# Eight result loads made in place and ahead of the last gate projections, in a hybrid mLSTM and differential-attention block

## The chip, the cores and the metric

The kernel runs on one core of one Trainium2 chip, as one launch. The metric is the device time of the whole program in microseconds (us). The three runs of the kernel before took 1701.33, 1698.94 and 1702.51 us; their median is 1701.33. All profile rows come from one more execution, taken by the hardware profiler.

## The reference, cut to what matters

One layer on a sequence of 1024 positions and a width of 1024, in float32. Two branches are computed from the same normalised input, each is gated, and their sum goes through an output projection:

```
proj = rmsnorm(x) @ w_in            # split into a_q, a_k, a_v, a_o, a_z, a_g, b_q, b_k, b_v, b_z, g_a, g_b
y_a  = rmsnorm(mlstm_fw + mlstm_bw) * sigmoid(a_o) * silu(a_z)          # branch A, 4 heads
y_b  = rmsnorm(diff_attention(rope(b_q), rope(b_k), b_v)) * silu(b_z)   # branch B, 8 heads
mix  = sigmoid(g_a + gb[0]) * (y_a @ w_branch_a) + sigmoid(g_b + gb[1]) * (y_b @ w_branch_b)
out  = rmsnorm(x + mix @ w_out)
```

The gates are the two sigmoids in front of the branch products. The kernel writes a sigmoid as a tanh of half its argument.

## The kernel before, in words

Every float32 matrix product is made of three products of rounded halves: each operand is held as a high part (written H, a rounded copy) and a low part (written L, the operand less its high part), and the products H·H, H·L and L·H are added up in PSUM. So every operand that comes from DRAM has to be split first: ScalarE copies it to H, and VectorE subtracts H from it to get L (for weights, GpSimd does the subtraction).

The work runs in stages. First the normalised input is split and stays in SBUF as hH and hL. Then come most input projections, the eight heads of branch B (whose results go to the DRAM tiles `yb`), and the four heads of branch A (whose results go to the DRAM tiles `ya`). The 16 gate projections, eight for each branch, are used as filler for TensorE throughout. One of them (`gate_units`) is two products of 24 matmuls, one for each half of the sequence; ScalarE takes each half's tanh from PSUM into the tile `gt`, of which there is one buffer (line 1547), and a DMA stores it to DRAM. PSUM holds two buffers `pj` for all these products, so a product can only start when the product two before it has been read by ScalarE or VectorE.

Three gate projections, called `rest`, are left when branch A's last head ends. The first five pieces of the 48 that they are cut into (a piece is three matmuls) run before that head's last transposes, the list `late`; seven more stand with `late`; then the pool w2 of branch A's heads is given back and the pool wy takes its place. From there the last 36 pieces are woven with eight calls of `load_y`, one for each of the eight 128-row tiles of branch B's result. A call loads a tile of 128 x 1024 float32 into a staging buffer `yraw` (two of them), ScalarE copies it to a slot H, and VectorE writes the low part to a slot L; both are slots of the tag `yb`, which has 16.

After the last gate product the memory of hH and hL is given back to the pool wr. Then pass B (`mix_units("gb")`) multiplies the eight loaded tiles with `w_branch_b`: 8 output tiles x 2 halves x 8 input tiles x 3 matmuls, input tile 0 first. VectorE multiplies each half by the gate, which is loaded back into `tgl`. Branch A's first four tiles are loaded by the same `load_y` into slots of the tag `r` in wr; branch A's last four go to slots of the tag `yb` that pass B has left. Pass A, the output projection and the last norm follow.

The order of TensorE's instructions is the program's order from here on (`keep(E.PE)`). The other engines' orders, and that of the DMA queue of SyncE (SP), are set by the planner, which puts an instruction where its own model of time has its operands ready, and of several ready ones takes the one that stands first in the program. Once built, each engine and each queue runs strictly in its order: an instruction that waits holds all behind it. Nearly every DMA of the kernel is issued by SP; six gate stores of the opening are issued by ScalarE. A tile of wy waits only for those tiles of w2 whose memory it takes.

Of the kernel before, what the change touches and what calls it, by code (L numbers as in the profile page):

```python
# [7 lines left out]
F32 = mybir.dt.float32  # L8
# [6 lines left out]
S = 1024  # L15
# [4 lines left out]
L = 256  # L20
# [25 lines left out]
class Unit:  # L46
# [5 lines left out]
    def __init__(self, cost, fn, keys=(), tag=None, hold=0.0, name=None, after=(), lane=0):  # L52
        self.cost, self.fn, self.keys = cost, fn, keys
        self.tag, self.hold, self.name, self.after, self.lane = tag, hold, name, after, lane
# [55 lines left out]
class Block:  # L110
    def __init__(self, tc, A):
        self.tc, self.nc, self.A = tc, tc.nc, A
        nc = self.nc
        self.v, self.a, self.p, self.t, self.q = nc.vector, nc.scalar, nc.gpsimd, nc.tensor, nc.sync
        self.wt = {}
        self.raws = {}
        self.ml, self.opening, self.ahead, self.terms, self.forms = False, True, False, {}, 0
        self.rs, self.tk, self.loaded = {}, {}, set()
        for n in ("w1", "w2", "wy", "wr"):
            setattr(self, n, _Late(self, "_" + n))  # L120
        self.gc = {}
# [709 lines left out]
    def gate_units(self, seg, i):  # L831
        key = ("w_in", OFF[seg] + 128 * i)
        idx = (0 if seg == "ga" else 8) + i

        def done(half, ps):
            t = self.wpool.tile([128, 512], F32, name="gt", tag="gt")
            self.a.activation(out=t, in_=ps, func=AF.Tanh, scale=0.5, bias=self.gbh[:, idx:idx + 1])
            (self.a if self.opening else self.q).dma_start(out=self.tg[seg][i][:, half * 512:(half + 1) * 512], in_=t)
        return sum((self.proj(key, half, lambda ps, half=half: done(half, ps)) for half in range(2)), [])


# [465 lines left out]
        return un, prev["O"](0) + prev["g"](1) + prev["scale"](4) + prev["scale"](6) + prev["O"](1)  # L1307


    def load_y(self, src, i, slot):  # L1310
        raw = self.wy.tile([128, S], F32, name="yraw", tag="yraw", bufs=2)
        self.q.dma_start(out=raw, in_=src[i])
        h, l = slot("H"), slot("L")
        self.a.copy(h, raw)  # L1314
        self.v.tensor_tensor(out=l, in0=raw, in1=h.bitcast(F32), op=ALU.subtract)  # L1315
        return h, l

    def slot(self, which, dt=F32R):
        pool, bufs = {"yb": (self.wy, 16), "mb": (self.wy, 8), "r": (self.wr, 16)}[which]
        return pool.tile([128, S], dt, name="sl_" + which, tag=which, bufs=bufs)  # L1320
# [108 lines left out]
    def build(self):  # L1429
# [19 lines left out]
        do = lambda f, cost=0.0: Unit(cost, f)  # L1449
        pool = lambda *x, **k: tc.tile_pool(*x, **k)  # L1450
        with pool(name="const", bufs=1) as self.const, \
# [32 lines left out]
            gq = [("gb", i) for i in range(8)] + [("ga", i) for i in range(8)]  # L1484
            fill = lambda m: sum((self.gate_units(*gq.pop(0)) for _ in range(m)), [])
# [16 lines left out]
            st3 = {}  # L1502
            w = Weaver()
            w.add(enter("h", "hpool"), enter("tab", "tab", side="right"), enter("tf", "tf", side="right"),
                  enter("p0", "p0", side="right"), banks("ps0", T=6), keep(E.PE, E.Activation, E.DVE, E.Pool), do(begin))
            k = self.PIECES
# [60 lines left out]
            w.add(enter("w2", "w2", side="right"), banks("ps2", T=2, SS=1, PO=1, I=1))  # L1567
            ml, late = self.ml_units([self.ml_head(n, stm[n]) for n in range(NH_A)], fill(2))
            w.add(do(lambda: setattr(self, "ml", True)), *ml)
            rest = fill(len(gq))  # L1570
            cut = len(rest) // 4
            w.add(*rest[:5])
            w.weave(late, rest[5:cut])
            w.add(do(lambda: setattr(self, "ml", False)), leave("ps2", "w2"), enter("wy", "wy", side="right"))
            yb = lambda x: self.slot("yb")
            loads = [do(lambda k=k: st3.__setitem__(("gb", k), self.load_y(self.yb, k, yb)), 1.0) for k in range(8)]
            w.weave(loads, rest[cut:])

            w.add(leave("h"), enter("wr", "wr"))
            passB = self.mix_units("gb", st3)  # L1580
# [1 line left out]
            loads = [do(lambda k=k: st3.__setitem__(("ga", k), self.load_y(self.ya, k, r)), 1.0) for k in range(4)]  # L1582
            w.add(*passB[:len(passB) // 2])
            w.weave(loads, passB[len(passB) // 2:])
            w.add(*[do(lambda k=k: st3.__setitem__(("ga", k), self.load_y(self.ya, k, yb))) for k in range(4, 8)])
            passA = self.mix_units("ga", st3)
            loads = [do(lambda k=k: self.load_wo(k, st3, "yb"), 1.0) for k in range(3)]
            k = len(passA) // 2
# [52 lines left out]
```

## Time and profile before

| | |
|---|---|
| median of 3 runs | 1701.33 us (1698.94 to 1702.51) |
| the profiled execution's own time | 1699.79 us |
| its span, first to last instruction | 1698.0 us |
| TensorE busy | 1650.1 us, 97% |
| mean granted TensorE clock | 0.996 |
| VectorE, ScalarE, GpSimd busy | 994.1, 760.0, 635.3 us |
| DMA | 178.79 MB, mean 105 GB/s |

Matmuls are pipelined and the profiler models their ends, so the distance from one start to the next is what counts: 0.227 us for a matmul of 512 columns at the full clock in the gate products and in pass B. PE is TensorE, PEld its weight loads, DVE VectorE, ACT ScalarE, POOL GpSimd; SPq and ACTq are the DMA issues of SyncE and ScalarE. Times in rows are us from the start of the span.

### The profile page before, as it was taken

The numbers are of one execution on the slowest core, as the hardware profiler recorded it, in microseconds if no ns is written. First come the engines' busy times: TensorE is split into PE (matmuls) and PEld (weight loads), VectorE is DVE, ScalarE is ACT, GpSimd is POOL, SyncE is SP. The second block draws the span as 40 slices with busy tenths as digits, with TensorE's granted clock in tenths as the row PEclk, the third lists the DMA queues.
The fourth block names the chain that finished last, engine by engine and source line by source line (L and its number), as shares of the span: only waits on it lengthen the run. The fifth ranks groups of instructions, "written<-read, shape, count | busy, mean of one in ns | idle before, by whom it ended". The sixth has DMA issues, their size and how long they took to land. (4 is left out here: it accounts for less than half of the span.)

```text
span 1698.0 us, 25367 instructions
## 1 busy us (share of the span) xinstructions
PE 1650.1 (97%) x9431; PEld 1387.7 (82%) x9431; DVE 994.1 (59%) x1799; ACT 760.0 (45%) x1522; POOL 635.3 (37%) x712
## 2 busy tenths in 40 slices
PE   7999999999999999999999999999999898999998
PEld 5777887887888988898888888889999777888887
DVE  5778668674277666766666765126666644135533
ACT  6454555543254454454445454325656644022221
POOL 5767676665343235424351431221331311212000
PEclk9999999999999999999999999999999999999999
DMA  5334434434231213221230221175554327344222
GB/s 179 101 118 134 137 115 134 124 124 137 75 81 44 63 38 87 63 63 37 76 88 26 63 75 63 50 208 155 143 170 140 104 93 244 119 142 136 87 92 83
DMA packets 175630, 178.79 MB, mean 105 GB/s; under 512 B 12185, under 2 KB 135410, under 8 KB 175506
## 3 DMA queue, kind: packets, MB, share of 16 engines
q1 hardware_dynamic: 174594, 175.58, 34.5%
q8 instruction: 74, 1.21, 0.3%
q10 hardware_dynamic: 912, 1.59, 0.2%
q14 instruction: 50, 0.41, 0.1%
HBM read 114.11 MB, written 46.24 MB: 94 GB/s over the span
## 5 line engine op out<-in xcount | busy, mean ns | idle before, releaser
L429 PE MATMUL pj<-hH,wH 128*128 128x512 f32 x640 | 266.3, 416 | 3.3 <-ACT f L542 1.5
L429 PE MATMUL pj<-hH,wL 128*128 128x512 f32 x640 | 251.9, 394 | 1.7 <-POOL wL L207 1.7
L429 PE MATMUL pj<-hL,wH 128*128 128x512 f32 x640 | 250.6, 392 | 0.2 <-DVE hL L580 0.2
L209 POOL TENSOR_TENSOR wL<-raw,wH 128x1024 fp32r<-128x1024 f32 x41 | 99.6, 2429 | 284.2 <-ACT wH L204 281.8
L928 ACT ACTIVATE e<-S,nm 128x1024 f32<-128x1024 f32 x128 | 142.7, 1115 | 134.2 <-DVE nm L926 133.9
L948 DVE TENSOR_TENSOR pL<-T,pH 128x512 fp32r<-128x512 f32 x128 | 87.9, 688 | 117.4 <-ACT pH L947 116.7
L926 DVE TENSOR_REDUCE nm<-S 128x1 f32<-128x1024 f32 x128 | 150.5, 1217 | 10.1 <-PE S L923 9.3
L429 PEld LDWEIGHTS pj<-hH,wH 128*128 128x128 f32 x640 | 120.7, 189 | 37.8 <-issue 14.4
L451 PE MATMUL pj<-wH,hH 128*128 128x256 f32 x512 | 149.9, 293 | 1.6 <-DVE vL L1035 1.3
L451 PE MATMUL pj<-wL,hH 128*128 128x256 f32 x512 | 144.9, 283 | 1.4 <-POOL wL L207 1.4
L429 PEld LDWEIGHTS pj<-hH,wL 128*128 128x128 f32 x640 | 120.4, 188 | 30.1 <-POOL wL L207 3.1
L451 PE MATMUL pj<-wH,hL 128*128 128x256 f32 x512 | 144.5, 282 | 0.0
L429 PEld LDWEIGHTS pj<-hL,wH 128*128 128x128 f32 x640 | 121.0, 189 | 18.2 <-DVE hL L580 0.6
L429 PE MATMUL pj<-sl_yb,wH 128*128 128x512 f32 x384 | 121.8, 397 | 4.7 <-ACT sl_yb L1314 2.1
L947 ACT CAST pH<-T 128x512 fp32r<-128x512 f32 x128 | 74.7, 584 | 100.5 <-PE T L131 99.9
L204 ACT CAST wH<-raw 128x1024 fp32r<-128x1024 f32 x56 | 58.8, 1050 | 126.8 <-PE pj L429 86.4
L923 PE MATMUL S<-kst,qq 64*128 64x512 f32 x768 | 106.5, 408 | 0.0
L451 PEld LDWEIGHTS pj<-wH,hH 128*128 128x128 f32 x512 | 97.7, 191 | 6.8 <-issue 3.9
L451 PEld LDWEIGHTS pj<-wL,hH 128*128 128x128 f32 x512 | 97.5, 190 | 2.3 <-POOL wL L207 2.3
L451 PEld LDWEIGHTS pj<-wH,hL 128*128 128x128 f32 x512 | 97.7, 191 | 0.1
L429 PEld LDWEIGHTS pj<-sl_yb,wH 128*128 128x128 f32 x384 | 73.3, 191 | 22.8 <-DVE sl_yb L1315 3.3
L934 DVE SCALAR_TENSOR_TENSOR e<-e,r,e 128x1024 f32<-128x1024 f32 x64 | 88.8, 1388 | 2.2
(358 smaller groups left out, 4099.9 us busy)
## 6 DMA issues: line engine op xcount, KB each, us to landing
raw<-in_w_in_dram SPq DMA_DIRECT2D x88, 512.0 KB, 3.8
kst<-hl SPq DMA_DIRECT2D x64, 128.0 KB, 2.4
qq<-hl SPq DMA_DIRECT2D x64, 128.0 KB, 2.4
x<-in_x_dram SPq DMA_DIRECT2D x8, 512.0 KB, 6.2
cak<-y SPq DMA_DIRECT2D x16, 256.0 KB, 2.3
cakH<-cin SPq DMA_DIRECT2D x16, 256.0 KB, 4.4
cakL<-tz SPq DMA_DIRECT2D x16, 256.0 KB, 4.0
gm<-oz SPq DMA_DIRECT2D x16, 256.0 KB, 2.8
```

The source lines that it names most:

```text
L204: self.a.copy(wH, raw)
L209: self.p.tensor_tensor(out=wL, in0=raw, in1=wHf, op=ALU.subtract)
L429: self.t.matmul(ps, lhsT=l[:, k, :], rhs=r, start=(n == 0), stop=(n == 23))
L451: self.t.matmul(ps[:, i, :], lhsT=l, rhs=r[:, k, :], start=(kh == 0 and k == 0 and m == 0), stop=(kh == 1 and k == 3 and m == 2))
L923: self.t.matmul(ps[:, o], lhsT=qq[r, x, c], rhs=k[r, y, o], start=(m == 0), stop=(m == 2))
L926: v.tensor_reduce(out=nm, in_=ps, axis=AX.X, op=ALU.max, negate=True)
L928: a.activation(out=e, in_=ps, func=AF.Exp, bias=nm[:, 0:1], accum_out=Z[:, j, t:t + 1])
L934: v.scalar_tensor_tensor(out=e0, in0=e, scalar=r[:, 0:1], in1=e0, op0=ALU.mult, op1=ALU.add)
L947: a.copy(pH[:, :, s], ps)
L948: v.tensor_tensor(out=pL[:, :, s], in0=ps, in1=pH[:, :, s].bitcast(F32), op=ALU.subtract)
```

## The change

`load_y` gets a form without staging: the DMA writes straight into the slot L (seen as plain float32), ScalarE copies from there to H, and VectorE subtracts in place. Branch B's eight loads and branch A's first four use it; branch A's last four keep the staging buffer. Branch B's eight loads now all stand ahead of the remaining pieces of `rest` instead of being woven among them. A flag `last`, set at the head of `rest`, makes ScalarE instead of SP issue the six stores of the last three gates; setting it is a unit of its own at the front of the list `rest`, which thus has 49 entries where it had 48, and is cut at the same places.

```diff
-        self.rs, self.tk, self.loaded = {}, {}, set()
+        self.rs, self.tk, self.loaded, self.last = {}, {}, set(), False
...
-            (self.a if self.opening else self.q).dma_start(out=self.tg[seg][i][:, half * 512:(half + 1) * 512], in_=t)
+            (self.a if self.opening or self.last else self.q).dma_start(out=self.tg[seg][i][:, half * 512:(half + 1) * 512], in_=t)
...
-    def load_y(self, src, i, slot):
-        raw = self.wy.tile([128, S], F32, name="yraw", tag="yraw", bufs=2)
-        self.q.dma_start(out=raw, in_=src[i])
-        h, l = slot("H"), slot("L")
+    def load_y(self, src, i, slot, direct=True):
+
+        if direct:
+            h, l = slot("H"), slot("L")
+            raw = l.bitcast(F32)
+            self.q.dma_start(out=raw, in_=src[i])
+        else:
+            raw = self.wy.tile([128, S], F32, name="yraw", tag="yraw", bufs=2)
+            self.q.dma_start(out=raw, in_=src[i])
+            h, l = slot("H"), slot("L")
         self.a.copy(h, raw)
         self.v.tensor_tensor(out=l, in0=raw, in1=h.bitcast(F32), op=ALU.subtract)
...
-            rest = fill(len(gq))
+            rest = [do(lambda: setattr(self, "last", True))] + fill(len(gq))
             cut = len(rest) // 4
             w.add(*rest[:5])
             w.weave(late, rest[5:cut])
...
-            w.weave(loads, rest[cut:])
+            w.add(*loads, *rest[cut:])
...
-            w.add(*[do(lambda k=k: st3.__setitem__(("ga", k), self.load_y(self.ya, k, yb))) for k in range(4, 8)])
+            w.add(*[do(lambda k=k: st3.__setitem__(("ga", k), self.load_y(self.ya, k, yb, False))) for k in range(4, 8)])
```

## Rows read from the trace of the kernel before

**Rows 1.** The page's busy times: engine, us, share of the span, instructions.

```profile
PE 1650.1 (97%) x9431; PEld 1387.7 (82%) x9431; DVE 994.1 (59%) x1799; ACT 760.0 (45%) x1522; POOL 635.3 (37%) x712
```

**Rows 2.** The chain that ended last: start, duration, what; the stretch around pass B's start.

```profile
1414.70 6.32 DMA yraw<-yb
...
1423.39 4.89 DMA yraw<-yb
...
1430.65 81.82 PE pj L429 x350
```

**Rows 3.** Timeline of TensorE: start, duration, line, operands, count; in brackets idle before, releaser.

```profile
1419.55 0.39 PE L429 MATMUL pj<-hH,wL 128*128 128x512 f32 x1
1420.90 0.72 PE L429 MATMUL pj<-sl_yb,wH 128*128 128x512 f32 x2 [0.96 <-ACT gt L837]
...
1424.90 0.39 PE L429 MATMUL pj<-sl_yb,wL 128*128 128x512 f32 x1
1426.27 0.49 PE L429 MATMUL pj<-sl_yb,wH 128*128 128x512 f32 x1 [0.99 <-ACT sl_yb L1314]
1427.53 0.50 PE L429 MATMUL pj<-sl_yb,wH 128*128 128x512 f32 x1 [0.76 <-DVE sl_yb L1315]
...
1429.39 0.80 PE L429 MATMUL pj<-sl_yb,wH 128*128 128x512 f32 x1 [1.13 <-ACT sl_yb L1314]
1430.65 0.80 PE L429 MATMUL pj<-sl_yb,wH 128*128 128x512 f32 x1 [0.46 <-DVE sl_yb L1315]
...
1436.36 0.63 PE L429 MATMUL pj<-sl_yb,wH 128*128 128x512 f32 x2
```

**Rows 4.** Stretches: length, busy us by engine (instructions), granted clock, DMA share, GB/s.

```profile
1425.00:1430.00 5.00, 2.12 (x6) 0.77 (x4) 1.85 (x2) 2.09 (x2) 0.62 (x1) 0.90 0.91 255
1430.00:1432.00 2.00, 1.54 (x4) 1.16 (x4) 0.69 (x2) 0.00 (x0) 0.00 (x0) 0.50 0.79 263
...
1436.00:1438.00 2.00, 2.00 (x11) 1.63 (x10) 0.99 (x1) 0.00 (x0) 0.00 (x0) 1.00 0.59 231
```

**Rows 5.** Timeline of ScalarE in the last two gate products.

```profile
1408.87 1.05 ACT L204 CAST wH<-raw 128x1024 fp32r<-128x1024 f32 x1 [2.95 <-PE pj L429]
...
1419.21 1.05 ACT L1314 CAST sl_yb<-yraw 128x1024 fp32r<-128x1024 f32 x1 [6.03 <-DMA yraw<-yb]
1420.16 0.68 ACT L837 ACTIVATE gt<-pj,gbh 128x512 f32<-128x512 f32 x1
```

**Rows 6.** Waits of SP's queue, 1396 to 1431 us: total, times, longest.

```profile
SPq L1312 <- DVE sl_yb L1315: 9.9, 8, 2.3
SPq L838 <- ACT gt L837: 6.9, 2, 5.8
```

**Rows 7.** Timeline of SP: the first load of branch B's results.

```profile
1398.23 0.37 SPq L1312 DMA_DIRECT2D yraw<-yb  x1
```

**Rows 8.** Instructions on tile yraw: duration ns min/median/max, first and last start.

```profile
L1314 ACT CAST sl_yb<-yraw x12: 1044/1052/1057, 1402.1 to 1518.3; 128x1024 fp32r<-128x1024 f32 x12
L1315 DVE TENSOR_TENSOR sl_yb<-yraw,sl_yb x12: 1211/1224/2635, 1403.2 to 1519.8; 128x1024 fp32r<-128x1024 f32 x12
```

**Rows 9.** Stretches again, for the DMA rate in the last column.

```profile
1406.00:1410.00 4.00, 4.00 (x19) 3.33 (x18) 1.17 (x1) 1.13 (x2) 0.00 (x0) 1.00 1.01 366
...
1398.00:1420.00 22.00, 21.93 (x97) 17.83 (x95) 6.22 (x4) 8.84 (x10) 4.80 (x2) 1.00 0.85 285
1414.00:1431.00 17.00, 12.70 (x50) 8.99 (x49) 5.57 (x5) 6.33 (x7) 2.49 (x1) 0.94 0.82 249
```

**Rows 10.** Instructions on tile gt in the opening: the stores that ScalarE issued.

```profile
L838 ACTq DMA_DIRECT2D tgb<-gt x6: 326/326/358, 25.0 to 60.9; - x6
```

**Rows 11.** Instructions on tile gt, 1395 to 1431 us: how long its stores took.

```profile
DMA to landing us min/median/max: 5.1/5.1/5.2
```

**Rows 12.** Timeline of TensorE at branch A's last transposes.

```profile
1386.07 0.39 PE L429 MATMUL pj<-hH,wL 128*128 128x512 f32 x1
1386.97 1.96 PE L131 MATMUL T<-ident,hm 128*128 128x128 f32 x8 [0.52 <-ACT hm L1216]
```

## The prediction, made before the change was run

> **What bounds the kernel now.** I read the page's busy times first: TensorE is busy 97% of the span [rows 1], so only time in which it waits or runs slowly can be won. The chain that ended last says where that is around this change: it is matmuls up to about 1409 us, then for some 20 us loads of `yraw` with their splits, then 82 us of matmuls without a break [rows 2]. So the loads of branch B's results end last at the start of pass B. The timeline of TensorE shows what this costs [rows 3]. The last gate matmul starts at 1419.55. The first matmul of pass B could follow 0.227 us later, at 1419.78 (0.227 is the distance of matmul starts at the full clock), but starts at 1420.90: its PSUM buffer was still to be read. Input tiles 0 to 5 run until 1424.90; tiles 6 and 7 come in four steps, each held by ScalarE's or VectorE's half of a split. From 1430.65 nothing waits, but the engine is on the lower of its two clock levels: the granted clock is 0.50 (1.2 GHz) in 1430 to 1432 and 1.00 (2.4 GHz) again in 1436 to 1438, behind a stretch of 5 us in which TensorE was busy for 2.12 [rows 4].
>
> **What the stall is worth.** Up to 1436.36, pass B has done 36 matmuls (24 of its first product and 4 x 3 of its second). At the full clock from 1419.78 they take 36 x 0.227 = 8.2 us and end at 1427.9. They ended 8.4 us later. That splits into 1.1 us for the PSUM buffer (1419.78 to 1420.90), 4.6 us in the steps for tiles 6 and 7 (1425.13 to 1430.65 is 5.5 us, in which four matmuls of 0.9 us together were started), 2.5 us by the low clock (from 1430.65 the 14 matmuls took 5.7 us, where 14 x 0.227 is 3.2), and 0.2 in slightly longer distances before. The size 8.4 is sure; the split matters only if a part of it stays.
>
> **Why the loads are late, and what the edits do to that.** Three holds stand in a ring. (1) Two `yraw` buffers: SP waited 9.9 us, in 8 waits, for VectorE to finish a split before it could issue the next load [rows 6]. (2) SP's order: gate stores stood among the loads, and SP waited 6.9 us in two of them for the tanh that they store [rows 6]. (3) ScalarE's order: the tanh of a gate product that ended at about 1414.3 stood behind a cast that waited 6.03 us for its load, and ran only at 1420.16 [rows 5]; that is the late PSUM buffer.
>
> Loads in place take hold (1) away: each of the eight has its own slot, so SP can issue them one after the other. Stores issued by ScalarE take (2) away. The first load was issued at 1398.23, in 0.37 us [rows 7], right behind branch A's last stores; from there eight issues take about 3 us, to 1401.3. Their bytes are 8 x 128 x 1024 x 4 = 4.2 MB. In front of them are branch A's last two stores (0.5 MB) and beside them, in ScalarE's row, up to three gate stores (0.8 MB): 5.5 MB. The weights and gates that pass B loads through SP stand behind them. For the rate I have 366 GB/s in the fullest 4 us, 285 over 1398 to 1420, and 249 over 1414 to 1431 [rows 9]; I take 285, because that stretch has this very mixture. 5.5 MB then take 19.3 us, to 1417.5; by 249 it is 22.1, to 1420.3, and by 366 it is 15.0, to 1413.2. Behind the last landing come one cast of 1.05 and one subtraction of 1.22 us [rows 8], the same in place as out of place by count of elements: the last tile is split at 1419.8 (1415.5 to 1422.6). It is wanted by the 22nd matmul of pass B, at 1419.78 + 21 x 0.227 = 1424.5. So even at the slowest rate the steps for tiles 6 and 7 go, and with them the fall of the clock.
>
> The PSUM buffer needs ScalarE to be in time. From 1398 to 1420 its work is eight casts (8.4 us), five tanhs of 0.68 (3.4), two weight casts (2.1) and five store issues of 0.33, the figure of the opening's six [rows 10], (1.7): 15.6 of 22 us. There is room, and since a product may use the buffer of the one two before, a tanh may be 5.4 us late (24 x 0.227) before TensorE notices. I cost ScalarE's stores at nothing on this ground; without that cover they would cost their 1.7 us. The one buffer `gt` makes a tanh wait until the last store has landed. On SP's crowded row stores took 5.1 us here [rows 11]; with 5.4 us between tanhs, and a tanh and an issue (1.0) before the store, the next tanh would then be late by 0.7 us, which the 5.4 of slack covers.
>
> The Trainium skill, page "DMA: Bandwidth & Descriptors", section "Issuing engines are not separate DMA queues", says that transfers issued by several engines run on the same 16 DMA engines, and that a second issuer only saves the issuing time. By that rule the stores' move would be worth five issues, under 2 us of SP's time, and nothing to the bandwidth. Rows 6 show that what SP lost there was not issuing time but a wait, which a later load had to sit out; the rule leaves that aside, and the trace decides.
>
> **What the edits cost.** Setting the flag is an entry of the list `rest`, and `rest[:5]` now holds four pieces where it held five. So TensorE reaches branch A's last transposes one piece, three matmuls or 0.68 us, earlier. There it already waited 0.52 us for ScalarE's scaling of `hm` [rows 12], whose chain of single steps this edit doesn't touch. The wait grows by 0.68 us, and the piece comes later: a loss of 0.7 us (0 if that chain gains for some reason; 1.7 if in addition one early cast of 1.05 stands in front of the scaling).
>
> Branch A's four loads in place now need the memory of hH and hL, and so wait in SP for the last gate matmul; behind them stand weights of pass B. Pass A starts some 85 us later, and a set of weights is used for 10.9 us, so I cost this at nothing; its cover is that the third set of weights is wanted only at about 1441.6. The second set was cast at 1408.87 [rows 5] and is wanted at 1430.7. Behind the loads its 0.5 MB lands at about 1419 to 1422, and with cast and subtraction it is ready some 4 us before it is wanted. After pass B's start everything hangs on TensorE, so what is won there is kept.
>
> **The sum.** -8.4 + 0.7 = -7.7 us. Against the profiled execution's own 1699.79 (span 1698.0, 1.79 around it) that is 1692.1. The median of the three runs is 1.5 above that execution; I take half of this into the forecast: 1692.9 us.
>
> **The rivals.** *The DMA rate, not the order, is the bound* (chance 0.17). For it: the 16 DMA engines were already busy 0.85 of 1398 to 1420 [rows 9]. If the planner puts the loads of two weight sets and two gates (2.1 MB) among them, 7.6 MB have to land first. At 285 GB/s the last tile lands at 1424.9 and is split at 1427.2, 2.0 us late with the 0.7 above: 1694.9, or 1697.4 if the clock falls again (2.5). At 249 it is split at 1431.0, as late as before: 1701 with the clock's fall. Against it: 366 GB/s were reached, and SP's order follows the program, where the loads come first. The Trainium skill's rule above, by which all issuers share the engines, would make this one likelier; rows 9 show room to 366.
>
> *The tanhs fall behind the casts* (0.12), the slower side. ScalarE runs in a fixed order. If the planner's model has all eight loads land early, it puts the eight casts, which now stand first in the program, ahead of the tanh of the product that ends at about 1403.5. On the chip that tanh then waits for the last load: 4.7 MB from 1398.2 at 285 GB/s, 1414.8, and 1416.6 with the cast and itself. The product that needs its PSUM buffer should start at 1409.6, so TensorE stands for 7.0 us and the clock falls (2.5): 9.5 us lost against 7.7 won, 1702.4 with the sum's base of 1700.6. At 249 GB/s it is 2.4 us more, 1704.8. It decides as soon as that tanh ends after 1414.8 (1409.6 + 7.7 - 2.5). For it: [rows 5] show a tanh 6 us behind a cast that waits. Against it: there the cast stood in its place by the program's weave; and loads that land one by one leave ScalarE idle in the planner's time too, when it takes the tanh.
>
> *The change doesn't do what it says* (0.09): the slots lie in memory that branch A's last tiles hold, the loads can't start before those are stored, and each later one waits in SP for its own; or the later stages wait for something else by then. About no change, 1700.5.
>
> **How the numbers follow.** The forecast has 0.62, by itself 1690 to 1695. A measurement of this kernel can tell 0.2%, or 3.4 us, from no change. Faster by more: 0.62 and two thirds of the first rival, 0.73. Slower by more: half of the second (its slow end) and a fifth of the third, 0.08. Within: the rest, 0.19. The range goes from 1689.8 (all of 8.4, also the wait of rows 12, on the lower base) to 1699.5, which takes in the first rival but for its end.
>
> **What would show it.** Right: eight load issues on SP without a wait between them, about 0.4 us apart; the first matmul of pass B 0.23 us behind the last gate matmul; no idle time in its first 24; a granted clock of 1.00 from 1415 to 1440; the wait at the transposes about 1.2 us. Wrong: a gate product that starts late behind a tanh, a cast that waits for a load while a tanh stands behind it, or pass B waiting for its seventh or eighth tile.

## The result, and the profile after

The changed kernel is slower: 1706.34 us median (six runs, 1704.48 to 1710.09) against 1699.77 (six runs of the kernel before, 1698.67 to 1702.51), ratio 1.0042, 95% interval [1.0032, 1.0052]. Its profiled execution took 1704.79 us, span 1703.0.

TensorE is busy 2.4 us longer than in [rows 1], with the same instructions; the rest of what it lost is idle time.

```profile
PE 1652.5 (97%) x9431; PEld 1389.5 (82%) x9431; DVE 992.9 (58%) x1799; ACT 760.7 (45%) x1522; POOL 634.7 (37%) x712
```

The chain that ended last (start, duration, what) has the shape of [rows 2], shifted: one more load of branch B's results, its split, then 80 us of matmuls. New is what stands in front of that load: DMA issues of SP.

```profile
1426.73 0.38 SPq L173
...
1427.22 0.53 SPq L1315
...
1427.79 6.04 DMA sl_yb<-yb
...
1433.85 1.05 ACT sl_yb L1320
...
1434.93 1.24 DVE sl_yb L1321
...
1436.21 80.63 PE pj L429 x350
```

The timeline of TensorE answers to [rows 12] with its first two lines and to [rows 3] with the others.

```profile
1385.18 1.96 PE L131 MATMUL T<-ident,hm 128*128 128x128 f32 x8 [1.19 <-ACT hm L1216]
1387.64 1.90 PE L131 MATMUL T<-ident,hm 128*128 128x128 f32 x8 [0.50 <-ACT hm L1216]
...
1419.90 0.39 PE L429 MATMUL pj<-hH,wL 128*128 128x512 f32 x1
1420.12 0.62 PE L429 MATMUL pj<-sl_yb,wH 128*128 128x512 f32 x2
...
1425.27 0.49 PE L429 MATMUL pj<-sl_yb,wH 128*128 128x512 f32 x1 [1.54 <-ACT sl_yb L1320]
1427.85 0.50 PE L429 MATMUL pj<-sl_yb,wH 128*128 128x512 f32 x1 [2.08 <-DVE sl_yb L1321]
...
1430.12 0.80 PE L429 MATMUL pj<-sl_yb,wH 128*128 128x512 f32 x1 [1.29 <-DVE sl_yb L1321]
...
1434.95 0.80 PE L429 MATMUL pj<-sl_yb,wH 128*128 128x512 f32 x1 [3.61 <-ACT sl_yb L1320]
1436.21 0.80 PE L429 MATMUL pj<-sl_yb,wH 128*128 128x512 f32 x1 [0.47 <-DVE sl_yb L1321]
...
1440.74 0.62 PE L429 MATMUL pj<-sl_yb,wH 128*128 128x512 f32 x2
```

I compare the two traces from a mark that lies ahead of the change, the last `PO` matmul of branch A's last head. It starts at 1381.27 before and at 1379.49 after (the difference, 1.8 us, came up earlier in the program, where nothing was changed; over all thirteen traces of this document the mark lies between 1379.49 and 1382.42). From there:

| stretch | before | after | difference |
|---|---|---|---|
| mark to the start of the last gate matmul | 38.28 | 40.41 | +2.13 |
| to the first matmul of pass B | 1.35 | 0.22 | -1.13 |
| to its 37th matmul | 15.46 | 20.62 | +5.16 |
| sum | 55.09 | 61.25 | +6.16 |

From the 37th matmul to the end it is 261.6 and 262.3 us. So the loss lies in this stage. The late PSUM buffer is gone, as predicted. Pass B lost 12.5 us against 36 x 0.227 = 8.2: 9.0 us of idle time, by the five brackets above, and some 3.5 us in longer distances between matmuls, most of it at the low clock.

Stretches of the trace (columns as in [rows 4]) show the clock. The granted clock falls in two places, behind the transposes and in pass B's waits.

```profile
1385.00:1390.00 5.00, 4.11 (x18) 3.23 (x19) 1.41 (x2) 2.92 (x8) 1.21 (x3) 0.77 0.53 171
1390.00:1395.00 5.00, 5.00 (x21) 4.03 (x21) 0.78 (x2) 0.69 (x1) 0.00 (x0) 0.89 0.49 166
...
1430.00:1435.00 5.00, 1.27 (x3) 0.55 (x3) 1.35 (x3) 2.09 (x2) 0.00 (x0) 0.50 0.99 390
```

Why the loads are late stands in SP's own timeline (`x3` is three issues in a row).

```profile
1396.19 0.37 SPq L1315 DMA_DIRECT2D sl_yb<-yb  x1
...
1401.95 0.38 SPq L173 DMA_DIRECT2D raw<-in_w_branch_b_dram  x1
1402.40 0.56 SPq L1315 DMA_DIRECT2D sl_yb<-yb  x1
...
1405.34 0.42 SPq L1315 DMA_DIRECT2D sl_yb<-yb  x1
...
1412.83 0.38 SPq L173 DMA_DIRECT2D raw<-in_w_branch_b_dram  x1
1413.26 1.52 SPq L1315 DMA_DIRECT2D sl_yb<-yb  x3
...
1415.45 0.74 SPq L1315 DMA_DIRECT2D sl_yb<-yb  x1
1426.73 0.38 SPq L173 DMA_DIRECT2D raw<-in_w_branch_b_dram  x1
...
1427.79 0.42 SPq L1315 DMA_DIRECT2D sl_yb<-yb  x1
```

The eight loads are not in a row: raw weight loads stand among them (and loads of gates and of branch A's results, not shown), and the last load stands behind three of those. What those wait for is the first line of SP's waits between 1395 and 1435 (total, times, longest), where [rows 6] had splits and tanhs. In the same list none of branch B's loads waits for memory or for a slot:

```profile
SPq L173 <- POOL wL L209: 19.9, 3, 8.9
```

A raw weight buffer comes free when GpSimd has split the weights before, and that waits for ScalarE's cast of them, as GpSimd's timeline shows for the third:

```profile
1424.35 2.36 POOL L209 TENSOR_TENSOR wL<-raw,wH 128x1024 fp32r<-128x1024 f32 x1 [11.55 <-ACT wH L204]
```

ScalarE's timeline closes the ring: the cast at 1423.24 stood behind casts of branch B's tiles that waited for their own loads, and behind a tanh.

```profile
1419.03 1.05 ACT L1320 CAST sl_yb<-sl_yb 128x1024 fp32r<-128x1024 f32 x1 [3.46 <-DMA sl_yb<-yb]
1420.63 1.05 ACT L1320 CAST sl_yb<-sl_yb 128x1024 fp32r<-128x1024 f32 x1 [0.55 <-DMA sl_yb<-yb]
1422.65 0.69 ACT L837 ACTIVATE gt<-pj,gbh 128x512 f32<-128x512 f32 x1 [0.97 <-DMA tga<-gt]
1423.24 1.04 ACT L204 CAST wH<-raw 128x1024 fp32r<-128x1024 f32 x1
```

Why did the planner put other DMAs between the loads? The theory: H and L are slots of one tag, and slots of a tag go out in the order in which the program first writes them: L0, H0, L1, H1. H of tile k goes out when its cast is planned, so a load that writes into L of tile k+1 can only be planned behind that cast, when the planner's model has tile k landed. Other DMAs that were ready took the places between. On the chip no load had to wait for the cast itself: the third was issued at 1405.34, ahead of the second tile's cast at 1407.95. What held the loads is the order that SP had been given. In the kernel before a load's target was `yraw`, a tag of its own. The planner's own steps are not on record; what the order of the slots does to the time is tested below.

### The profile page after: what moved, and what is told of

Its sections match the earlier page's. It is cut to its first block, busy times and chain, and to the rows that moved or that the text cites. A ratio compares the mean times of both kernels' runs of the same rounds, so it can differ in the third digit from the quotient of the medians.

```text
span 1703.0 us, 25363 instructions
## 1 busy us (share of the span) xinstructions
PE 1652.5 (97%) x9431; PEld 1389.5 (82%) x9431; DVE 992.9 (58%) x1799; ACT 760.7 (45%) x1522; POOL 634.7 (37%) x712
```

## The experiments

| kernel | loads | slots H, L | calls | gate stores | shift | ratio to before, 95% interval | median us |
|---|---|---|---|---|---|---|---|
| changed | in place | one tag | ahead | ScalarE | yes | 1.0042 [1.0032, 1.0052] | 1706.34 |
| e3_cut | in place | one tag | ahead | ScalarE | no | 1.0042 [1.0030, 1.0054] | 1705.90 |
| e9_direct_woven | in place | one tag | woven | SP | no | 1.0027 [1.0017, 1.0037] | 1702.91 |
| e4_shift | staged | one tag | woven | SP | yes | 1.0005 [0.9996, 1.0013] | 1699.89 |
| e5_stores | staged | one tag | woven | ScalarE | no | 1.0001 [0.9992, 1.0010] | 1698.55 |
| e7_ahead | staged | one tag | ahead | SP | no | 0.9983 [0.9974, 0.9992] | 1696.74 |
| e1_l_first | in place | L first | ahead | ScalarE | yes | 1.0001 [0.9992, 1.0009] | 1698.74 |
| e13_tags_cut_sp | in place | two tags | ahead | SP | no | 1.0001 [0.9993, 1.0010] | 1699.27 |
| e11_tags | in place | two tags | ahead | ScalarE | yes | 0.9978 [0.9969, 0.9986] | 1695.46 |
| e10_woven_splits | in place | L first | splits woven | ScalarE | no | 0.9968 [0.9956, 0.9981] | 1693.94 |
| e14_tags_woven | in place | two tags | woven | ScalarE | no | 0.9968 [0.9957, 0.9980] | 1693.84 |
| e12_tags_cut | in place | two tags | ahead | ScalarE | no | 0.9961 [0.9950, 0.9973] | 1692.12 |

"Shift" is the flag's entry at the front of `rest`, which moves one piece behind the transposes. The kernel before took 1698.77 us beside e1, e3, e11 and e12, 1699.00 beside e4, e5, e9 and e13, and 1699.42 beside e7, e10 and e14.

**The slots (e11).** The changed kernel with H and L under tags of eight slots each, and nothing else:

```diff
-        pool, bufs = {"yb": (self.wy, 16), ...}[which]
+        if which == "yb":
+            self.forms += 1
+            which = "ybH" if self.forms % 2 else "ybL"
+        pool, bufs = {"ybH": (self.wy, 8), "ybL": (self.wy, 8), ...}[which]
...
-            yb = lambda x: self.slot("yb")
+            self.forms = 0
+            yb = lambda x: self.slot("yb" + x)
```

> The changed kernel with nothing but the slots' tags changed: the 16 slots of branch B are 8 for H and 8 for L, instead of 16 of one tag; the program's order of load, cast and subtraction is as in the change. Slot order theory: the same eight load issues in a row on SP, and casts and tanhs in turn on ScalarE, so no wait at pass B's start and none in the gate products: 6.3 us below the kernel before (8.4 won, 2.1 lost at the transposes), 1693.5 us. DMA rate rival: as slow as the change, or at best as the kernel before: 1700 or more. If instead the program's order (loads behind the casts of the tiles before) was the cause, this kernel is as slow as the change, 1706.

1695.46 us, 10.9 less than the changed kernel and faster than the one before; that is 2 us above the theory's 1693.5, and below both rivals (1700 and 1706). SP issues all eight loads in a row, in 6.3 us, and pass B has no wait for a tile. The later users of the tag `yb` get the two tags too, but what follows pass B's 37th matmul takes 261.9 us, against 262.3 in the changed kernel. So the slots' order under one tag is the cause.

```profile
1398.48 6.34 SPq L1315 DMA_DIRECT2D sl_ybL<-yb  x8
```

**The slots in another way (e1).** One tag of 16, but the eight L slots are taken and loaded first, then come the eight splits, ahead of the gates (`take_y` takes L and loads into it, `split_y` takes H, casts and subtracts):

```diff
+            loads = [do(lambda k=k: st3.__setitem__(("lb", k), self.take_y(self.yb, k, yb)), 1.0) for k in range(8)]
+            loads += [do(lambda k=k: st3.__setitem__(("gb", k), self.split_y(st3["lb", k], yb))) for k in range(8)]
```

> The changed kernel with branch B's eight slots L and their eight loads first, and behind them the eight slots H with cast and subtraction; slots of one tag are then handed out L0 to L7, H0 to H7. Slot order theory: in the changed kernel the planner gave slot L of tile k+1 only behind slot H of tile k, so it planned load k+1 behind cast k, and let SP take loads of weights in between, whose wait held the rest. Here SP issues the eight loads one after the other from about 1396, and pass B finds all tiles split: no wait for the splits of tiles 5 to 7, 12.5 us less of the loss there, less what the casts cost: the planner now puts all eight in front of the tanh of the gate product that ends at 1409, so that TensorE may wait up to 3 us in a gate product. 1694 to 1697 us. DMA rate rival: eight loads at once, beside stores and weights, land no earlier than one by one; tiles 5 to 7 are late again and the time is 1700 or more.

The loads go out in a row here too (from 1396.75, in 6.5 us) and pass B waits for no tile, so the loads came out as the theory has it. The time is a miss: 1698.74 where it had 1694 to 1697, that of the kernel before. ScalarE's timeline has the reason: eight casts stand ahead of a tanh, behind a tanh that waited 8.35 us for the one buffer `gt` (its count is set in line 1467 of the kernel before, not in 1547).

```profile
1400.77 0.35 ACTq L838 DMA_DIRECT2D tga<-gt  x1
1409.09 0.69 ACT L837 ACTIVATE gt<-pj,gbh 128x512 f32<-128x512 f32 x1 [8.35 <-DMA tga<-gt]
...
1411.18 7.68 ACT L1318 CAST sl_yb<-sl_yb 128x1024 fp32r<-128x1024 f32 x8
1418.76 0.68 ACT L837 ACTIVATE gt<-pj,gbh 128x512 f32<-128x512 f32 x1
```

TensorE's timeline shows the price in a gate product, ahead of pass B; the granted clock behind it, in 1420 to 1425, is 0.74:

```profile
1419.50 0.79 PE L429 MATMUL pj<-hH,wH 128*128 128x512 f32 x1 [3.89 <-ACT gt L837]
```

**L first, splits woven (e10).** As e1 with the splits woven among the gates, and the cuts of `rest` one entry later, so that no piece moves.

> The slot order mended in another way: one tag of 16 slots as in the changed kernel, but all eight L slots are taken and loaded first, ahead of the gates, and the eight splits (H slot, cast, subtraction) are woven among the gates; stores by ScalarE, no shift. Against the run that took L first with all splits ahead of the gates (1698.7, its tanhs behind casts that wait). Theory (the order of the slots and of casts against tanhs is all that counts, not the tags): 1691 to 1694, ratio 0.995 to 0.997, no wait of TensorE over 0.5 us between the transposes and 1445. Rival (with the loads issued in one burst ScalarE's stores land so late that the one gt buffer stops TensorE whatever the casts' place): a wait for gt of 2 to 4 us and the clock's fall behind it, 1696 to 1699.

1693.94 us, in the theory's range, but TensorE still waited for a `gt` 1.9 us in two times, 1.1 the longest, without the clock's fall. Both theories had that wait wrong. One tag is no harm where L goes out first. Of the 4.8 us between e1 and e10 a part is the shift, which e10 leaves out and which is worth 3.3 us between e11 and e12; the rest goes with the casts' place, to which e1's wait of 3.9 us points.

**The shift in the changed kernel (e3).**

```diff
-            w.add(*rest[:5])
-            w.weave(late, rest[5:cut])
+            w.add(*rest[:6])
+            w.weave(late, rest[6:cut + 1])
...
-            w.add(*loads, *rest[cut:])
+            w.add(*loads, *rest[cut + 1:])
```

> The changed kernel with the cut of the list of gate pieces moved by one, so that five pieces stand again before branch A's last transposes and twelve before the loads; all else as changed. Theory (two costs): of the 6.2 us lost between the tanh at 1382.0 and pass B's 36th matmul, 2.1 are the missing piece: 0.7 of wait and 1.4 of the low clock that the longer idle time brings. This kernel gets those back: 1704.2 us where the change took 1706.3, the first transpose 0.5 us behind the last piece, and the granted clock at 1.00 in the 10 us behind the transposes; pass B waits as long as in the changed kernel. Rival (all of the loss is at pass B's start, and the fall of the clock at the transposes is only displaced): no difference from the change, 1706.

A miss: no gain, which is the rival's number. The loss at the transposes is gone (waits of 0.53 and 0.50 us, granted clock 1.00 in 1385 to 1395), and from the mark to pass B it takes 38.5 us, but its 36th matmul starts 23.5 us later, against 20.4 in the changed kernel: the last load lands at about the same time (its cast starts at 1434.28, in the changed kernel at 1433.85). TensorE's waits for tiles are not longer (8.8 us in seven times, 9.0 in the changed kernel), but its matmuls between and behind them are slower: the granted clock is 0.53, 0.50, 0.50 and 0.76 in the four stretches from 1425 to 1445, where the changed kernel has 0.87, 0.50, 0.61 and 1.00.

```profile
1435.00:1440.00 5.00, 4.16 (x9) 2.97 (x10) 4.27 (x4) 2.42 (x3) 0.00 (x0) 0.50 0.08 30
1440.00:1445.00 5.00, 5.00 (x18) 3.96 (x18) 0.00 (x0) 0.00 (x0) 0.00 (x0) 0.76 0.00 0
```

**The shift by itself (e4).** The kernel before with `rest = [do(lambda: None)] + fill(len(gq))`.

> The kernel before with one empty unit in front of the list rest and nothing else: one piece (three matmuls) fewer ahead of branch A's last transposes. Theory (the loss at the transposes lies beside the wait for the loads, and only the longer of the two counts): the loads of the kernel before end at 1430 whatever TensorE does before, so the ratio is 1.0000 to 1.0008, about 1699.5 if the kernel before takes 1699. Rival (the two losses add up): 2.1 us slower, ratio 1.0012, 1701.1. Both expect at the transposes a wait of about 1.7 us in two steps and a granted clock of about 0.77 in the 5 us behind them, where the kernel before has 0.5 us and 1.00; the theory alone expects pass B's 36th matmul no more than 0.7 us later.

Within 0.2%. The ratio doesn't part the two theories (the rival's 1.0012 lies in the interval), but the trace does, though it is that of the slowest of the eleven runs (1701.33): the transposes lose (1.19 and 0.44 us of waiting, granted clock 0.71 in 1390 to 1395), pass B's first matmul comes 40.3 us behind the mark instead of 39.6, and its 36th 0.7 us later, as the theory has it, and not 2.1.

**The shift where no load is late (e12).** e11 with e3's cuts.

> The tags of the last kernel and the cut moved by one as in the first. If the two costs are separate they add up: 8.4 us below the kernel before, 1691.4 us, granted clock 1.00 from 1380 to 1450. If the clock would have fallen in either place anyway (one cost hidden behind the other), it is nearer to 1693.5.

1692.12 us, the fastest kernel here. Against e11 it is 3.3 us by the medians, and 1.5 us from the mark to the 36th matmul in the two traces (48.66 and 47.21). So the shift counts where the loads don't bind; where they do, e3 and e4 show no effect that is clear of the noise. Between 1380 and 1445 TensorE's waits are those at the transposes, which the kernel before has too, 0.7 us on another line of the last head, and one of 0.2 for a `gt`:

```profile
PE T L131 <- ACT hm L1216: 1.0, 2, 0.5
PE T L131 <- ACT W L1183: 0.7, 1, 0.7
PE pj L429 <- ACT gt L837: 0.2, 1, 0.2
```

**In place alone (e9).** The kernel before with the in-place form of `load_y` alone.

> The kernel before with loads in place as the only edit: woven among the gates as before, stores issued by SP, no shift. Theory (H and L share one tag, whose slots are given out in the program's order, so that load k+1 is ordered behind cast k): the loads stay a chain, one at a time, and the last one is issued behind a raw weight load; slower than the kernel before by 4 to 7 us, 1703 to 1706 if that takes 1699, and pass B waits for its seventh or eighth tile until about 1435. Rival (freeing the loads of the staging buffers helps by itself, the harm came from putting them all ahead of the gates): 1692 to 1696.

Slower, by 4.6 us by the ratio, at the low end of the theory's range. Waits for a tile, 6.6 us in six times, stand in pass B. What stands between the loads is not the same as in the changed kernel: SP waited 11.0 us for the tanhs whose stores stood among them, and 4.1 for raw buffers. SP's timeline has the last load late again, behind a raw weight load:

```profile
1423.78 0.38 SPq L173 DMA_DIRECT2D raw<-in_w_branch_b_dram  x1
...
1424.84 0.42 SPq L1315 DMA_DIRECT2D sl_yb<-yb  x1
```

**The place of the calls alone (e7).** The kernel before with `w.add(*loads, *rest[cut:])` in place of the weave.

> The kernel before with the place of the loads as the only edit: all eight calls ahead of the remaining gates, still through two staging buffers, stores by SP, no shift. Theory (the harm lay in the slots' order, which a load into a staging buffer doesn't meet): each load still waits for the split two before it and for SP's gate stores, so the loads end about where they did; ratio 0.999 to 1.002, 1697 to 1702 if the kernel before takes 1699. Rival (putting the calls ahead of the gates is itself what made it slower, as casts come in front of tanhs): 1.003 and more, 1704 to 1708, with TensorE waiting for a gt of ScalarE before 1420.

Faster, just below the theory's range (its end is 0.999, and the interval reaches 0.9992), and on the other side than the rival. SP waits 3.0 us for tanhs instead of 6.9 and 7.1 for splits instead of 9.9 [rows 6]. Pass B starts late (2.25 us behind a `gt`) but then waits once, 0.65 us. Why the place alone helps is not shown beyond that.

**The stores alone (e5).** The kernel before with the flag set by a unit of its own ahead of `rest`, so that no piece moves.

> The kernel before with the six stores of the last three gates issued by ScalarE and nothing else: staged loads, woven, no shift. Theory A (SP's waits for the tanhs held the loads, rows 6): SP loses its 6.9 us of waiting, the last load is issued some 3 to 6 us earlier, and pass B's steps shrink; 3 to 6 us faster, 1693 to 1696 if the kernel before takes 1699. Theory B (the two staging buffers bind, and the stores' place is hidden by them): ratio 0.9994 to 1.0006, and SP's waits for VectorE's splits grow from 9.9 us by what the others shrink. I hold B a little likelier, 0.55 to 0.45, since each load took 5 to 6 us and only two could be under way.

No change in the time, as theory B has it. Its profiled execution was the slowest of its eleven (1702.97), so I read only the kinds of wait from it: those for tanhs are gone, and waits for landings in `yraw` and for raw buffers stand in their place. Those for the splits did not grow, so theory B had the place of the waits wrong.

```profile
SPq L173 <- POOL wL L209: 10.1, 3, 4.3
SPq L1312 <- DVE sl_yb L1315: 9.8, 7, 2.3
SPq L1312 <- DMA yraw<-yb: 9.1, 2, 4.8
```

**The stores in company (e13).** e12 with the gate stores on SP.

> The fastest kernel so far (loads ahead, H and L slots under tags of their own, no shift; 1692.1) with the gate stores issued by SP instead of ScalarE. Theory (the stores' issuer matters by the order that it leads to: with SP issuing, all eight casts stand ahead of the tanh of the product that ends at about 1404, so that TensorE must wait for it in the gate products): 4 to 9 us slower than that kernel, 1696 to 1701, TensorE idle for 3 to 7 us before 1420 behind a gt of ScalarE, pass B without a wait for a tile. Rival (the issuer saves issuing time alone, six times 0.3 us on another engine): within 1 us of it, 1691 to 1693.

6.8 us slower than e12 by the ratios (0.0040 of 1699), as the theory has it. SP issued the eight loads from 1397.81 and the store of the tanh of 1398.30 behind them, at 1402.25; ScalarE ran all eight casts ahead of the next tanh, and TensorE stood for it:

```profile
1412.49 1.04 ACT L1320 CAST sl_ybH<-sl_ybL 128x1024 fp32r<-128x1024 f32 x1 [0.21 <-DMA sl_ybL<-yb]
1413.45 0.68 ACT L837 ACTIVATE gt<-pj,gbh 128x512 f32<-128x512 f32 x1
```

```profile
1414.18 0.79 PE L429 MATMUL pj<-hH,wH 128*128 128x512 f32 x1 [5.77 <-ACT gt L837]
```

That the planner put the tanh there because `gt` was held until its store had its turn on SP is argued, not shown. The Trainium skill, page "DMA: Bandwidth & Descriptors", section "Issuing engines are not separate DMA queues", gives a second issuer only the saved issuing time. The runs agree for e5 (no change) and differ here, since the issuer also sets the order of everything behind the store.

**The weave with free slots (e14).** e12 with the calls woven again.

> The fastest kernel so far (1692.1) with its eight calls woven among the gates again, as in the kernel before; H and L slots under tags of their own, stores by ScalarE, no shift. Theory (once the slots are free of each other the loads go out in a row wherever their calls stand): within 1.5 us of that kernel, 1691 to 1694, ratio 0.995 to 0.997, the eight loads issued within 8 us. Rival (standing ahead of the gates is a needed part): the last load is issued 10 us later or more and pass B waits again: 1695 to 1700.

1693.84 us, in the theory's range; the loads went out within 8.9 us, where it had 8 (five, a raw weight load, three). The intervals of e10, e12 and e14 overlap; standing ahead of the gates is not needed.

## Why the prediction was wrong

The step that failed is "Loads in place take hold (1) away: each of the eight has its own slot, so SP can issue them one after the other." Each had a slot of its own, but not from the start: in the planner's order it got it in its turn, behind the cast of the tile before. I counted the buffers and not the order in which one tag hands them out. The eight issues are spread over 31.6 us (1396.19 to 1427.79). e11, which changes the slots' tags alone, has them in a row (6.3 us, where I said about 3); e9 shows that the in-place form by itself brought 4.6 us of loss by the ratio, where the whole change brought 7.1.

Two more sentences fall with that step: that the weights of pass B "stand behind them", and that "SP's order follows the program, where the loads come first". Three raw weight loads stood among the eight, and SP waited 19.9 us for their buffers. This hold could be seen in the kernel before: in the very window of [rows 6] it cost SP as much as the tanhs did, and I left it out of the ring.

```profile
SPq L173 <- POOL wL L209: 6.9, 3, 4.4
```

"Slower by more" had a chance of 0.08, for two reasons that are not the one that held. The third rival, "the loads can't start", came nearest, but it named the memory of branch A's last tiles, and priced it at no change: I had not seen that a load out of its turn also waits for the weights that go ahead of it.

- *The size of the stall* (8.4 us) was nearly right. e12, without the shift, needs 7.7 us less from the mark to the 36th matmul (47.21 against 54.86), and 6.6 less by the ratio. The change as I had imagined it is e11: 1695.46, within the range, 2.6 above the forecast; by the ratio it won 3.7 us where I had 7.7, and from the mark to the 36th matmul 6.2.
- *The PSUM buffer*: right, 1.1 us came back.
- *The shift*, 0.7 us, was mis-sized: the wait grew by 0.67 us as predicted (1.19 for [rows 12]'s 0.52), but the clock fell behind it, and the stretch lost 2.1 us. In the changed kernel it cost nothing that the runs could tell all the same (e3), since it lay beside the longer wait for the loads.
- *ScalarE's stores at nothing*: right alone (e5), wrong in company: with the loads ahead and free they are worth 6.8 us (e13).
- *Branch A's four loads at nothing*: what follows pass B's 37th matmul took 0.6 us longer (262.26 against 261.64), less than one run differs from another.
- *The DMA rate as the bound*: refuted. In e12 the last load was issued at 1405.0 and the longest landing took 10.2 us, so all bytes were there by 1415.2; I had 1417.5 at 285 GB/s.
- *The tanhs behind the casts*: not in the changed kernel, where the loads came too late for it, but in e1 and e13. I priced it at 1702.4; both came out at 1.0001 of the kernel before. The stall in e13 was 5.8 us where I had 7.0.

What stays open: how the planner came to each order; and e3 is slower than e9 by 0.0015, and whether the place of the calls or the stores' issuer does that was not tried apart.

## What to carry to other kernels

A load that writes into its final buffer takes that buffer's place in the order of its tag: before staging is removed, list the order in which the tag hands its buffers out and what stands between two load targets; give the targets a tag of their own or take them first. List all holds of the queue, also those that look small: here the one left out grew from 6.9 to 19.9 us. Where several holds form a ring, one edit alone may show nothing or harm (stores 0, in place +0.27%, place -0.17%), and the same edits with the slots mended and the shift removed give -0.39%. An empty entry in a list that is cut by index moves work, and what that costs can lie hidden until the rest is mended.

## What the runs showed of the hardware

ScalarE's stores of 256 KB landed in 2.6 to 5.8 us in the changed kernel, but mostly slower beside the eight loads in a row (5.6 to 6.0 in e12, 2.8 to 7.3 in e11, and most in e1). These lines are of the tile `gt` between 1395 and 1435 us, in the changed kernel:

```profile
DMA to landing us min/median/max: 2.6/3.0/5.8
```

and in e1, where [rows 11] had 5.1 on SP:

```profile
DMA to landing us min/median/max: 6.1/7.1/8.2
```

With one `gt` buffer the next tanh can't start before the landing: in e1 one waited 8.35 us for it. DMA also moved more than the 366 GB/s of [rows 9], in e12:

```profile
1405.00:1410.00 5.00, 5.00 (x24) 4.14 (x23) 2.76 (x3) 2.87 (x4) 0.00 (x0) 1.00 1.03 415
1410.00:1415.00 5.00, 5.00 (x23) 3.89 (x21) 3.34 (x3) 2.55 (x4) 0.00 (x0) 1.00 1.06 395
```

The Trainium skill, page "DMA: Bandwidth & Descriptors", section "Where 436 GB/s comes from", says that for transfers between HBM and SBUF the HBM side binds, at about 358 GB/s for one of the two cores that share it; these stretches of a single core are above that, and the measurement decides.

Behind the transposes the granted clock fell to 0.50 to 0.53 in a stretch of 2 us in all four traces with a first wait of 1.2 us (the changed kernel, e1, e4, e11), and in two of the nine with 0.5 us (e5 and e7, of which the kernel before is not one). So that fall is not tied to the shift alone.
